# Attention in numbered slots with a written engine order, GLU and branch work moved beside it, and SSM rotations from short tables

## The chip, the cores and the metric

One core of a Trainium2 chip runs the whole kernel. Its engines run side by side, each in the order of its own instruction list: PE (TensorE, matmuls and transposes, with its weight loads shown as PEld), DVE (VectorE), ACT (ScalarE), POOL (GpSimd) and SP, which issues most transfers. The metric is device time in microseconds; a lower time is better. Three runs of the kernel before gave 1538.99 to 1541.56 us, median 1540.11 us.

## The reference, cut to what matters

One decoder layer on 1024 tokens with 16 meta tokens in front (1040 rows of 1024 numbers):

```
xn = RMSNorm(h)
[q | k | v | u | gate_a | gate_b] = xn @ W_in
a  = stick-breaking attention(q, k, v)          8 heads x 64, strictly causal
s  = GLU(S5 complex-diagonal SSM(u))            32 groups x 16 channels, state 64
h += (sigmoid(gate_a) * (a @ W_pa) + sigmoid(gate_b) * (s @ W_pb)) @ W_o
h += hierarchical MoE(RMSNorm(h))               top-1 of 4 groups, then top-2 of 8 experts
```

The attention weight of key s for query t is `sigmoid(z[t,s])` times the product of `1 - sigmoid(z[t,j])` over the keys j between them, with `z = q.k / 8`. The SSM state turns by a fixed complex factor at each step; the kernel works on chunks of 8 tokens (130 chunks), and needs the cosines and sines of 129 multiples of an angle for each state.

## The kernel before

**Numbers.** A matrix product is taken in three passes: each operand is split into a rounded part and the rest (`h` and `l`), and `mm3` (L131) issues `wh*xh`, `wh*xl` and `wl*xh` for each block of 128 contraction rows (L134 to L136). `split` (L101, L102) makes the two parts, the first on ACT, the second on DVE.

**Stages.** The program's order is: norms and transposes of x; the projection of u; the SSM in four blocks of 8 groups (`ssm`); four pairs of heads (`att_proj`, `att_pair`); GLU and the two branches; the output projection with the router; the MoE; the final norm. The gate projections (`gates`, 16 units of 128 columns, two steps of 24 matmuls each) depend on nothing but xn and serve as filler. `weave` alternates two generators by count: 21 gate steps (`SF`) beside the SSM, then projections of the next head pair and 3, 3 and 2 gate steps beside a pair of heads. Beside the last pair stand the GLU steps. This is the order in which instructions are recorded; a list scheduler then places them on each engine by its own estimate of when each could run, so neighbours in the code need not be neighbours on the engine.

**SSM.** For each block POOL builds the tables `RC` and `RS` (128 partitions x 8 groups x 129) by doubling: seven rounds of six passes (L549 to L554). DVE makes `GT` and `ET` (L558 to L563), PE turns them and multiplies the inputs (L598), DVE rotates the result by `RC`, `RS` (L600 to L603), scans it (L606) and, with POOL (L608), rotates it back (L609 to L611); PE forms the output (L618, L620).

**Attention.** A head takes its queries in four groups (j = 0 to 3) of two blocks of 128. For a block, PE computes the logits in chunks of up to 512 columns with two matmuls each: L745 with `kh`, L746 with `kl`. Both contract over 128 rows: `qs` holds a head's rounded queries in its own 64 rows and the rests in the other 64, and `kh` and `kl` hold the head's 64 rows twice. ACT takes two sigmoids of a chunk (L748, L749), POOL masks the last 128 columns (L751), DVE scans the products (L754) and POOL multiplies (L755). PE turns the weights in blocks (L770), ACT and DVE split them (L780, L781), PE multiplies by the values (L790; L785 in the last pair, which works in plain f32). The 16 meta tokens are a block of their own, so its value matmuls contract over 16 rows.

Of the kernel before, what the change touches and what calls it, by code (L numbers as in the profile page):

```python
# [44 lines left out]
SF, MF, GP = 21, 3, (3, 3, 2)  # L45
# [7 lines left out]
def _f(ap):  # L53
    return ap.bitcast(F32)
# [19 lines left out]
def tile_block(ctx, tc, i, out):  # L74
# [16 lines left out]
    attn_d = dr.tile([512, S], F32, name="attn_d")  # L91
    gate_d = dr.tile([2 * D, S], F32, name="gate_d")
# [46 lines left out]
    with ExitStack() as ca:  # L139
# [21 lines left out]
        with ExitStack() as cx:  # L161
# [5 lines left out]
            def proj(col, chunks, evac):  # L167
                h, l = load_w([win[:, :, col:col + 128]])
                for n0, n1 in chunks:
                    t = ps.tile([128, 512], F32, name="mm", bufs=2)  # L170
                    for k in range(KD):
                        mm3(t[:, :n1 - n0], h[:, k, :], l[:, k, :], xh[:, k, n0:n1], xl[:, k, n0:n1], k == 0, k == KD - 1)
                    evac(t, n0, n1)
                    yield

# [94 lines left out]
            aq = [None, pool(c3, "aq1", bufs=2)]  # L270
            cq = ExitStack()
            aq[0] = pool(cq, "aq0", bufs=2)
            st = {}
            drain(islice(gen, MF), att_proj(tc, ap, aq[0], ps, proj, ident, 0, st))
            for hp in range(3):
                pair = att_pair(tc, ap, ps, ident, hp, st, attn_d)
                fill = chain(att_proj(tc, ap, aq[(hp + 1) % 2], ps, proj, ident, hp + 1, st), islice(gen, GP[hp]))
                weave(pair, fill, 16, 8 + GP[hp])
                drain(fill, pair)
            dst = []  # L280
            pair = att_pair(tc, ap, ps, ident, 3, st, attn_d, dst)
            next(pair)
            drain(gen)
            cq.close()


        with ExitStack() as c4:
            c5 = ExitStack()
            p = pool(c5, "br", side="right")
            ah, al, sh, sl = (p.tile([128, 4, S], F32R, name=n) for n in ("ah", "al", "sh", "sl"))  # L290
            with ExitStack() as c6:
                nc.sync.dma_start(gb, i["glu_b"])
                at = pool(c6, "glu", bufs=2, side="right")
                gl = glu(tc, at, ps, i, load_w, mm3, split, gb, y_d, sh, sl)

                def loads():
                    for k in range(3):
                        a = wp.tile([128, 2, 512], F32, name="wr", bufs=2)
                        nc.sync.dma_start(a, attn_d[k * 128:k * 128 + 128])
                        split(ah[:, k], al[:, k], a.rearrange("p a b -> p (a b)"))  # L300
                        yield
                dst += ah, al
                weave(pair, chain(gl, loads()), 16, 18)
                drain(pair, gl)
# [25 lines left out]
            wa = i["w_branch_attn"].rearrange("(k p) c -> p k c", p=128)  # L330
            wb = i["w_branch_ssm"].rearrange("(k p) c -> p k c", p=128)
            w0 = load_wo(0)
            p = pool(c5, "gat", side="right", bufs=2)
            for m in range(KD):
                h, l = load_w([wb[:, :, m * 128:m * 128 + 128], wa[:, :, m * 128:m * 128 + 128]])
                T2 = []
                for q in range(2):
                    c = slice(q * 512, q * 512 + 512)
                    t = ps.tile([128, 512], F32, name="qk", bufs=2)
                    for k in range(4):  # L340
                        mm3(t, h[:, k, :], l[:, k, :], sh[:, k, c], sl[:, k, c], k == 0, k == 3)
                    T2.append(t)
                for q in range(2):
                    c = slice(q * 512, q * 512 + 512)
                    ga = p.tile([128, 512], F32, name="ga")
                    gb = p.tile([128, 512], F32, name="gb")
                    nc.sync.dma_start(gb, gate_d[D + m * 128:D + m * 128 + 128, c])
                    nc.sync.dma_start(ga, gate_d[m * 128:m * 128 + 128, c])
                    V.tensor_mul(gb, gb, T2[q])
# [4 lines left out]
                    P.tensor_add(ga, ga, gb)  # L354
# [15 lines left out]
def ssm_prep(tc, p, i, bcast, out):  # L370
# [72 lines left out]
    t1, t2 = W("t1", (128, 4, G)), W("t2", (128, 4, G))  # L443
# [18 lines left out]
    for _ in range(3):  # L462
# [4 lines left out]
        V.tensor_scalar(s, wi, 2.0, None, op0=OP.mult)  # L467
    yield
# [22 lines left out]
    X, X2, C1, C2, BA, BB, u1 = (W(n, (128, G, CH)) for n in ("X", "X2", "C1", "C2", "BA", "BB", "u1"))  # L491
# [20 lines left out]
    out.update(c=c, s=s, Lr=Lr, Li=Li, d8=d8, BA=BA, BB=BB, C1=C1, C2=C2, sg=sg, nsg=nsg, dd=dd)  # L512


def ssm(tc, p, ps, ident, u_d, y_d, prep):
    nc = tc.nc
    V, A, P = nc.vector, nc.scalar, nc.gpsimd
    c, s, Lr, Li, d8, BA, BB, C1, C2, sg, nsg, dd = (
        prep[n] for n in ("c", "s", "Lr", "Li", "d8", "BA", "BB", "C1", "C2", "sg", "nsg", "dd"))
# [4 lines left out]
    N = NCH - 1  # L524
    for blk in range(4):
# [12 lines left out]
        RC, RS = W("RC", (128, 8, N), bufs=2), W("RS", (128, 8, N), bufs=2)  # L538
        P.memset(RC[:, :, 0:1], 1.0)
        P.memset(RS[:, :, 0:1], 0.0)  # L540
        P.tensor_copy(RC[:, :, 1], c[:, gs])
        P.tensor_copy(RS[:, :, 1], s[:, gs])
        ta, tb = W("ta", (128, 8, 64)), W("tb", (128, 8, 64))
        n = 1
        while n < 128:
            br, bi = (x[:, :, n:n + 1].to_broadcast([128, 8, n]) for x in (RC, RS))
            ar, ai = RC[:, :, 1:n + 1], RS[:, :, 1:n + 1]
            a, b = ta[:, :, :n], tb[:, :, :n]
            P.tensor_mul(a, ai, bi)  # L549
            P.tensor_mul(b, ar, br)  # L550
            P.tensor_sub(RC[:, :, n + 1:2 * n + 1], b, a)
            P.tensor_mul(a, ar, bi)
            P.tensor_mul(b, ai, br)
            P.tensor_add(RS[:, :, n + 1:2 * n + 1], a, b)  # L554
            n *= 2
        yield
        GT, tmp, ET = W("GT", (128, 8, T + 1, CH), bufs=2), W("tmp", (128, 8, T + 1, CH)), W("ET", (128, 8, T, CH), bufs=2)
# [14 lines left out]
        KP = W("KP", (CH, 8, 2, 128))  # L572
        P.memset(KP[:, :, 0], 0.0)
        for g0 in (0, 4):
# [4 lines left out]
            A.copy(KP[:, g0:g0 + 4, 1], tp[:CH])  # L579
        dg = W("dg", (CH, 8, CH))  # L580
        V.tensor_mul(dg, dd[:, gs, None].to_broadcast([CH, 8, CH]), ident[:CH, None, :CH].to_broadcast([CH, 8, CH]))
        V.tensor_add(KP[:, :, 1, 0:CH], KP[:, :, 1, 0:CH], dg)
        M = W("M", (128, 8, 128), bufs=2)
        KPf = KP.rearrange("p g a b -> p g (a b)")
        for ti in range(T):
            nc.sync.dma_start(M[ti * CH:ti * CH + CH], KPf[:, :, 128 - CH * ti:256 - CH * ti])
# [45 lines left out]
def glu(tc, p, ps, i, load_w, mm3, split, gb, y_d, sh, sl):  # L632
    nc = tc.nc
    V, A, P = nc.vector, nc.scalar, nc.gpsimd
    yh = p.tile([128, 4, S], F32R, name="yh", bufs=1)
    yl = p.tile([128, 4, S], F32R, name="yl", bufs=1)
    yd = y_d.rearrange("f t c -> f (t c)")

    def load(k, q):
        y = p.tile([128, 512], F32, name="y", bufs=2)  # L640
        nc.sync.dma_start(y, yd[k * 128:k * 128 + 128, q * 512:q * 512 + 512])
        return y

    for k in range(4):
# [757 lines left out]
```

## Time and profile before

| | us |
|---|---|
| median of three runs | 1540.11 |
| the profiled execution: its own time | 1539.6 |
| the profiled execution: its span | 1537.7 |
| SSM beside gate projections | 73.2 to 262.9 |
| head pairs | 262.9 to 653 |
| branches | to 725 |
| output projection, router, MoE, final norm | 725 to 1537.7 |

PE is recorded as busy in 1456.8 us (95%) of the span, DVE in 63%, ACT in 47%, POOL in 34%. A matmul's recorded duration runs on into the next one's, so busy time alone says little: the distance between the starts of two equal neighbours is what one costs. The granted clock is 1.0 at 2.4 GHz; a stretch with a mean below that was partly at 1.2 GHz.

### The profile page before, as it was taken

Reading aid. Unit: us, or ns where it says so; the run is one execution under the profiler, and the core shown is the slowest. Engines: PE = TensorE matmul, PEld = TensorE weight load, DVE = VectorE, ACT = ScalarE, POOL = GpSimd, SP = SyncE. Lnnn points to the kernel's source line nnn. Section 1 sums busy time; section 2 is a strip of 40 time slices with the busy share of each in tenths; the row PEclk is TensorE's granted clock in tenths of the full one; section 3 lists DMA queues with packets and bytes.
Section 4 is the critical chain, followed back from the end, with each engine's and each line's share of the span. In section 5 each row is a group of like instructions: output and inputs, shape, how many; then the busy total and the mean of one; then the engine's idle time right before and its main releaser. Section 6 shows DMA issues by size and latency. Waiting matters only on the chain. (4 is left out here: it accounts for less than half of the span.)

```text
span 1537.7 us, 19509 instructions
## 1 busy us (share of the span) xinstructions
PE 1456.8 (95%) x6900; PEld 1123.4 (73%) x6900; DVE 963.0 (63%) x1488; ACT 722.3 (47%) x1141; POOL 518.9 (34%) x542
## 2 busy tenths in 40 slices
PE   7989799999999989999998799999999999999986
PEld 6967688998888867778787566666666666666663
DVE  6757565465756568665578566666665566656547
ACT  6212122455656577432223255555555455555543
POOL 1199941144444465332255321111111111111034
PEclk8999899999999999999999799999999999999998
DMA  8242344211111015264763799999999989999754
GB/s 256 77 104 72 92 104 97 60 42 54 30 51 34 28 44 142 78 198 160 268 247 124 286 346 356 352 354 353 356 360 351 353 342 358 334 334 357 271 200 163
DMA packets 132197, 314.77 MB, mean 205 GB/s; under 512 B 24305, under 2 KB 82289, under 8 KB 107522
## 3 DMA queue, kind: packets, MB, share of 16 engines
q1 hardware_dynamic: 120898, 295.99, 55.0%
q0 software_dynamic: 9728, 16.83, 2.9%
q8 instruction: 55, 0.90, 0.2%
q10 hardware_dynamic: 1472, 0.69, 0.2%
q14 instruction: 44, 0.36, 0.1%
HBM read 284.03 MB, written 44.11 MB: 213 GB/s over the span
## 5 line engine op out<-in xcount | busy, mean ns | idle before, releaser
L134 PE MATMUL mm<-xh,wh 128*128 128x512 f32 (+4 forms) x608 | 224.1, 369 | 1.1 <-DVE kl L691 0.6
L135 PE MATMUL mm<-xl,wh 128*128 128x512 f32 (+4 forms) x608 | 222.6, 366 | 0.0
L136 PE MATMUL mm<-xh,wl 128*128 128x512 f32 (+4 forms) x608 | 221.3, 364 | 0.8 <-DVE wl L102 0.8
L1159 POOL DMA_INDIRECT ye_d<-w,tab x32 | 56.1, 1754 | 250.0 <-ACT w L1152 249.4
L134 PEld LDWEIGHTS mm<-xh,wh 128*128 128x128 f32 x608 | 115.4, 190 | 16.0 <-issue 1.1
L136 PEld LDWEIGHTS mm<-xh,wl 128*128 128x128 f32 x608 | 115.4, 190 | 14.9 <-DVE wl L102 1.5
L135 PEld LDWEIGHTS mm<-xl,wh 128*128 128x128 f32 x608 | 115.3, 190 | 13.9 <-DVE xl L225 0.4
L754 DVE TENSOR_TENSOR_SCAN pr<-pr 128x144 f32<-128x144 f32 (+3 forms) x64 | 92.6, 1448 | 46.8 <-POOL pr L751 46.1
L102 DVE TENSOR_TENSOR w<-m,w 128x2048 fp32r<-128x2048 f32 x38 | 88.9, 2342 | 40.8 <-ACT w L101 40.7
L102 DVE TENSOR_TENSOR w<-r,w 128x2048 fp32r<-128x2048 f32 x36 | 82.2, 2291 | 47.6 <-ACT w L101 47.2
L1066 POOL DMA_INDIRECT w<-hg_d,tab x31 | 34.8, 1122 | 222.0 <-PE tr L1088 217.1
L755 POOL TENSOR_TENSOR be<-be,pr 128x143 f32<-128x143 f32 (+3 forms) x64 | 89.4, 1400 | 38.4 <-DVE pr L754 36.0
L1120 PE MATMUL a<-r,xf 128*128 128x512 f32 x224 | 100.7, 592 | 0.0
L1120 PE MATMUL a<-m,xf 128*128 128x512 f32 x208 | 93.3, 592 | 0.0
L1128 DVE SCALAR_TENSOR_TENSOR mid<-a,tab,mid 128x512 f32<-128x512 f32 x64 | 47.9, 749 | 63.8 <-ACT mid L1126 52.0
L101 ACT CAST w<-r 128x2048 fp32r<-128x2048 f32 x38 | 72.1, 1903 | 27.5 <-PE a L1113 14.4
L101 ACT CAST w<-m 128x2048 fp32r<-128x2048 f32 x38 | 72.5, 1907 | 18.9 <-PE o L1146 10.3
L101 ACT CAST wh<-wr 128x1024 fp32r<-128x1024 f32 (+1 forms) x44 | 44.6, 1014 | 65.8 <-PE mm L135 57.3
L1120 PEld LDWEIGHTS a<-r,xf 128*128 128x128 f32 x224 | 41.8, 190 | 42.3 <-issue 40.4
L102 DVE TENSOR_TENSOR wl<-wr,wh 128x1024 fp32r<-128x1024 f32 (+1 forms) x44 | 57.1, 1297 | 23.6 <-ACT wh L101 23.5
L1146 PE MATMUL o<-w,w 128*128 128x512 f32 x172 | 68.6, 399 | 3.2 <-DVE w L102 3.2
L751 POOL TENSOR_SCALAR_AFFINE_SELECT pr<-pr 128x128 f32<-128x128 f32 x64 | 26.3, 411 | 132.9 <-ACT pr L748 113.1
(534 smaller groups left out, 3766.2 us busy)
## 6 DMA issues: line engine op xcount, KB each, us to landing
r<-in_w_dram SPq DMA_DIRECT2D x84, 1024.0 KB, 7.9
m<-in_w_dram SPq DMA_DIRECT2D x82, 1024.0 KB, 8.1
x<-in_w_dram SPq DMA_DIRECT2D x26, 1024.0 KB, 7.9
wr<-in_w_in_dram SPq DMA_DIRECT2D x32, 512.0 KB, 4.2
gate_d<-gt SPq DMA_DIRECT2D x32, 256.0 KB, 2.3
x<-in_x_dram SPq DMA_DIRECT2D x8, 512.0 KB, 4.6
y<-y_d SPq DMA_DIRECT2D x16, 256.0 KB, 3.2
wr<-in_w_out_dram SPq DMA_DIRECT2D x8, 512.0 KB, 4.3
```

The source lines that it names most:

```text
L101: a = (A if heng is None else heng).copy(h, src)
L102: return a.ins, (V if leng is None else leng).tensor_sub(l, src, _f(h)).ins
L134: nc.tensor.matmul(ps, lhsT=wh, rhs=xh, start=first, stop=False)
L135: nc.tensor.matmul(ps, lhsT=wh, rhs=xl, start=False, stop=False)
L136: nc.tensor.matmul(ps, lhsT=wl, rhs=xh, start=False, stop=last)
L754: V.tensor_tensor_scan(rv, rv, rv, 1.0, op0=OP.mult, op1=OP.bypass)
L755: P.tensor_mul(be[:, :W - 1], be[:, :W - 1], pr[:, 1:W])
L1066: q = P.indirect_dma_start(out=xg[e % XG], out_offset=None, in_=hg_d, in_offset=IO(ap=tab[:, e, 0:1] if e else rt["idx"], axis=0), bounds_ ...
L1120: nc.tensor.matmul(a[w], lhsT=xf[:, k], rhs=raws[n][:, k], start=False, stop=(k == 3))
L1128: V.scalar_tensor_tensor(s, a[n], r, s, op0=OP.mult, op1=OP.mult)
L1146: nc.tensor.matmul(o[n], lhsT=hh[:, kk], rhs=l[:, k, cs], start=False, stop=False)
L1159: put = P.indirect_dma_start(out=ye_d, out_offset=IO(ap=tab[:, e, 1:2], axis=0), in_=y, in_offset=None, bounds_check=2 * S - 1, oob_is_err ...
```

## The change

- **Rotations.** Two short tables of powers (17 and 9 entries for all 32 groups) are made once on DVE (`powers`); each block's `RC` and `RS` of 9 x 16 entries are their products: three passes on POOL and three on DVE. The block matrix `M` is loaded above its diagonal blocks only, into two pages cleared at the start.
- **Filler.** 20 gate steps stand beside the SSM instead of 21.
- **Slots.** Attention, GLU and the remaining gates are recorded by `attention` in 122 slots (numbers -10 to 111; the 112 from 0 on handle one block of value matmuls each). In a slot PE turns the next block, computes up to two logit chunks, takes a quota of filler and multiplies a block by the values; ACT, DVE and POOL work on what the slots before have left (`later`). Inside `manual_schedule` the four engines keep the recorded order; SP does not belong to it.
- **Plan.** GLU runs in slots -3 to 8 beside the first heads and leaves its result in DRAM (`s_d`); projections and gates fill slots up to 97; in slot 98 the pages of xn are given up and `s_d`, `attn_d` are read back into pages made there; slots 104 to 111 take the SSM half of two of the eight branch units.
- **Keys.** `kl` holds each head's 64 rows once; the second logit matmul contracts over these 64 rows alone, with the rounded queries.

```diff
-SF, MF, GP = 21, 3, (3, 3, 2)
+SF = 20
+AHEAD = 2
...
+        plan = [((-10, -4), [unit_qkv(0, 2)]), ((-3, 8), [unit_glu(m) for m in range(4)]), ((9, 24), qkv(1)),
+                ((25, 52), [unit_gate(10)] + qkv(2)), ((53, 80), [unit_gate(m) for m in (11, 12)] + qkv(3)),
+                ((81, 97), [unit_gate(m) for m in (13, 14, 15)]), ((104, 111), [unit_branch(m) for m in range(AHEAD)])]
...
+            for k in range(4):
+                sl.later(1 + k, lambda k=k: load_s(s_d, *late["s"], k, 128))
+            for k in range(4):
+                sl.later(6 + k, lambda k=k: load_s(attn_d, *late["a"], k, 128 if k < 3 else 64))
...
+        with tc.manual_schedule(engines={mybir.EngineType.PE, mybir.EngineType.Activation, mybir.EngineType.DVE, mybir.EngineType.Pool}):
+            attention(heads, sl, range(-10, 112), quota, fill, {98: merge_pages}, attn_d)
...
+    pb = powers("pb", 16, c, s)
+    pa = powers("pa", 8, pb[0][:, :, 16], pb[1][:, :, 16])
...
-        while n < 128:
-            br, bi = (x[:, :, n:n + 1].to_broadcast([128, 8, n]) for x in (RC, RS))
-            ar, ai = RC[:, :, 1:n + 1], RS[:, :, 1:n + 1]
-            a, b = ta[:, :, :n], tb[:, :, :n]
-            P.tensor_mul(a, ai, bi)
-            P.tensor_mul(b, ar, br)
-            P.tensor_sub(RC[:, :, n + 1:2 * n + 1], b, a)
...
+        for eng, R, t, x, y, op in ((V, RS, tb, (ar, bi), (ai, br), OP.add), (P, RC, ta, (ar, br), (ai, bi), OP.subtract)):
+            eng.tensor_mul(R, *x)
+            eng.tensor_mul(t, *y)
+            eng.tensor_tensor(R, R, t, op=op)
...
-                        nc.tensor.matmul(z[:, :c1 - c0], lhsT=q, rhs=k1[e][:, c0:c1], start=True, stop=False)
-                        nc.tensor.matmul(z[:, :c1 - c0], lhsT=q, rhs=k2[e][:, c0:c1], start=False, stop=True)
...
+        nc.tensor.matmul(z[:, :c1 - c0], lhsT=q, rhs=self.k1[e][:, c0:c1], start=True, stop=False)
+        nc.tensor.matmul(z[:, :c1 - c0], lhsT=q[own], rhs=self.k2[own, c0:c1], start=False, stop=True)
...
+        sl.later(1, sigmoids)
+        if last:
+            sl.later(2, scan)
...
+    for x in slots:
+        sl.now = x
+        if x in at:
+            at[x]()
+        store = None
+        if 0 <= x + 1 < len(blocks):
+            s, b = blocks[x + 1]
+            h, e, j = steps[s]
+            store = h.turn(e, j, b)
+        sl.run()
+        if store:
+            store()
+            w[x + 1] = h.w
+        for h, *z in zs.get(x, []):
+            h.logits(*z, sl)
+        for _ in range(quota.get(x, 0)):
+            next(fill)
+        if 0 <= x < len(blocks):
+            s, b = blocks[x]
+            h, e, j = steps[s]
+            h.values(e, j, b, w.pop(x))
```

POOL's list in the SSM stage before: the last round of doubling of the first block's tables (`ta`, `tb` are scratch), then the next block's first passes.

```order
L549 TENSOR_TENSOR ta_932<-RS_927 128x512
L550 TENSOR_TENSOR tb_933<-RC_926 128x512
L551 TENSOR_TENSOR RC_926<-tb_933,ta_932 128x8x64
L552 TENSOR_TENSOR ta_932<-RC_926,RS_927 128x512
L553 TENSOR_TENSOR tb_933<-RS_927,RC_926 128x512
L554 TENSOR_TENSOR RS_927<-ta_932,tb_933 128x8x64
L549 TENSOR_TENSOR ta_1300<-RS_1295 128x8
L550 TENSOR_TENSOR tb_1301<-RC_1294 128x8
```

POOL's list in the same stage now; `par`, `pai`, `pbr`, `pbi` are the short tables, `R` with `St` the rotation back of a block's scan.

```order
L668 TENSOR_TENSOR RC_983<-par_554,pbr_524 128x1152
L668 TENSOR_TENSOR RC_1275<-par_554,pbr_524 128x1152
L669 TENSOR_TENSOR ta_985<-pai_555,pbi_525 128x1152
L670 TENSOR_TENSOR RC_983<-RC_983,ta_985 128x1152
L628 TENSOR_TENSOR u1_607<-X_603,fi_581 128x512
L669 TENSOR_TENSOR ta_1277<-pai_555,pbi_525 128x1152
L670 TENSOR_TENSOR RC_1275<-RC_1275,ta_1277 128x1152
L669 TENSOR_TENSOR ta_1575<-pai_555,pbi_525 128x1152
L722 TENSOR_TENSOR R_1138<-St_1140,RC_983 128x1032
```

42 table passes of a block have become three, and the second block's tables stand ahead of the first block's rotation.

PE's list before, where the third head pair ends: logit chunks (`qk`) stand between value matmuls (`pv`) and transposes (`tr`) where the scheduler put them.

```order
L745 MATMUL qk_5840<-kh_4739,qs_4737 128x264
L746 MATMUL qk_5840<-kl_4741,qs_4737 128x264
L790 MATMUL pv_5633<-wth_5676,V_3722 128x256
L745 MATMUL qk_5929<-kh_4739,qs_4737 128x328
L746 MATMUL qk_5929<-kl_4741,qs_4737 128x328
L790 MATMUL pv_5633<-wtl_5677,V_3722 128x256
L790 MATMUL pv_5633<-wth_5676,V_3722 128x256
```

PE's list now, one slot among the first heads: the last transposes of a block, two logit chunks, filler.

```order
L914 MATMUL tr_2889<-ident_60,be_2631 128x128
L914 MATMUL tr_2889<-ident_60,be_2680 128x128
L880 MATMUL qk_2914<-kh_2151,qs_2149 128x272
L881 MATMUL qk_2914<-kl_2152,qs_2149 128x272
L880 MATMUL qk_2919<-kh_2151,qs_2149 128x400
L881 MATMUL qk_2919<-kl_2152,qs_2149 128x400
L136 MATMUL mm_2932<-xh_85,wh_2834 128x512
L137 MATMUL mm_2932<-xl_86,wh_2834 128x512
```

The row of L881 now lies alone between matmuls over 128 rows, in all 112 logit chunks of the program.

PE's list now in slots 99 to 101, where the plan has no filler.

```order
L880 MATMUL qk_6182<-kh_4899,qs_4897 128x456
L881 MATMUL qk_6182<-kl_4900,qs_4897 128x456
L880 MATMUL qk_6185<-kh_4899,qs_4897 128x456
L881 MATMUL qk_6185<-kl_4900,qs_4897 128x456
L946 MATMUL pv_6154<-wth_6143,V_4901 128x128
L914 MATMUL tr_6189<-ident_60,be_5977 128x128
L914 MATMUL tr_6189<-ident_60,be_6016 128x128
```

Before, the GLU's matmuls stood among the chunks of these last heads.

## Rows read from the trace of the kernel before

**Rows 1.** The page's first part: busy us, share of the span, instructions.

```profile
PE 1456.8 (95%) x6900; PEld 1123.4 (73%) x6900; DVE 963.0 (63%) x1488; ACT 722.3 (47%) x1141; POOL 518.9 (34%) x542
```

**Rows 2.** Busy time by stage: length, each engine's busy us, clock, DMA.

```profile
73.20:262.90 189.70, 171.48 (x854) 140.76 (x854) 120.31 (x156) 41.98 (x65) 134.37 (x197) 0.94 0.41 97
262.90:540.00 277.10, 274.32 (x1616) 241.56 (x1614) 168.56 (x251) 156.20 (x378) 109.14 (x132) 1.00 0.15 42
540.00:660.00 120.00, 110.10 (x551) 85.52 (x550) 84.10 (x93) 73.87 (x181) 60.32 (x63) 0.97 0.31 91
660.00:726.00 66.00, 66.00 (x292) 54.25 (x291) 40.74 (x62) 17.17 (x35) 18.84 (x15) 1.00 0.55 176
870.00:1480.00 610.00, 604.72 (x2378) 413.21 (x2376) 367.81 (x252) 340.91 (x312) 92.73 (x65) 1.00 0.90 337
```

**Rows 3.** PE's waits in the SSM stage: us in total, times, longest.

```profile
PE qk L618 <- DVE R L611: 11.3, 2, 10.0
PE qk L598 <- DVE mm__1124 L602: 6.9, 1, 6.9
```

**Rows 4.** Busy time in 20 us of the SSM stage.

```profile
100.00:120.00 20.00, 13.06 (x59) 10.46 (x59) 8.26 (x14) 1.17 (x2) 18.12 (x36) 0.77 0.37 77
```

**Rows 5.** POOL's costliest lines, 60 to 263 us: busy us, mean ns, idle before.

```profile
L551 POOL TENSOR_TENSOR RC<-tb,ta 128x8 f32<-128x8 f32 (+6 forms) x28 | 21.6, 773 | 2.0
...
L552 POOL TENSOR_TENSOR ta<-RC,RS 128x8 f32<-128x8 f32 (+6 forms) x28 | 16.6, 593 | 2.0
L608 POOL TENSOR_TENSOR R<-St,RC 128x1032 f32<-128x1032 f32 x4 | 11.6, 2911 | 35.7 <-DVE St L606 35.7
```

**Rows 6.** DVE lines, 54 to 263 us.

```profile
L600 DVE TENSOR_TENSOR R<-qk,RC 128x387 f32<-128x387 f32 (+1 forms) x12 | 6.1, 510 | 14.3 <-POOL RC L551 8.5 <-PE qk L598 5.7
...
L560 DVE TENSOR_TENSOR GT<-GT,tmp 128x1152 f32<-128x1152 f32 x4 | 5.9, 1474 | 0.0
...
L398 DVE SCALAR_TENSOR_TENSOR ea<-ea,eq 128x32 f32<-128x32 f32 x12 | 2.3, 191 | 0.1
```

**Rows 7.** PE in order of time: start us, us, line, contracted*output rows, form.

```profile
472.06 0.40 PE L134 MATMUL mm<-xh,wh 128*128 128x512 f32 x1
472.29 0.40 PE L135 MATMUL mm<-xl,wh 128*128 128x512 f32 x1
472.62 0.38 PE L790 MATMUL pv<-wth,V 16*128 16x256 f32 x1
472.93 0.50 PE L136 MATMUL mm<-xh,wl 128*128 128x512 f32 x1
473.26 0.40 PE L134 MATMUL mm<-xh,wh 128*128 128x512 f32 x1
```

**Rows 8.** PE's weight loads in the same stretch.

```profile
472.06 0.19 PEld L135 LDWEIGHTS mm<-xl,wh 128*128 128x128 f32 x1
472.62 0.18 PEld L790 LDWEIGHTS pv<-wth,V 16*128 16x128 f32 x1 [0.36 <-issue]
```

**Rows 9.** PE in order of time, value matmuls over 128 rows, then transposes.

```profile
466.99 0.28 PE L790 MATMUL pv<-wth,V 128*128 128x256 f32 x1
467.11 0.28 PE L790 MATMUL pv<-wtl,V 128*128 128x256 f32 x1
...
467.63 1.36 PE L770 MATMUL tr<-ident,be 128*16 128x128 f32 x11
```

**Rows 10.** Weight loads of the second logit matmul, 263 to 660 us.

```profile
L746 PEld LDWEIGHTS qk<-kl,qs 128*128 128x128 f32 x112 | 21.4, 192 | 0.9
```

**Rows 11.** ACT lines of the attention, 263 to 660 us, shapes apart.

```profile
L101 ACT CAST wh<-wr 128x1024 fp32r<-128x1024 f32 x18 | 19.0, 1056 | 12.1 <-PE mm L135 10.8 <-issue 1.2
...
L748 ACT ACTIVATE pr<-qk 128x456 f32<-128x456 f32 x16 | 8.9, 557 | 4.3 <-PE qk L746 4.1
L748 ACT ACTIVATE pr<-qk 128x392 f32<-128x392 f32 x16 | 8.1, 505 | 1.8 <-POOL be L755 0.8 <-PE pv L790 0.5 <-PE qk L746 0.4
...
L778 ACT COPY wth<-tr 128x512 f32<-128x512 f32 x12 | 6.7, 576 | 6.6 <-PE tr L770 6.6
```

**Rows 12.** The page's DMA issues: count, KB each, us to landing.

```profile
wr<-in_w_in_dram SPq DMA_DIRECT2D x32, 512.0 KB, 4.2
```

## What the change should do to the time

> **What bounds the kernel now.** I read the page's first part, then busy time by stage, then in the stages where PE is not full the waits, then single instructions in order of time. The first part names PE: recorded as busy in 1456.8 of 1537.7 us, with DVE next at 963.0 [rows 1]. A matmul's record runs on into its successor, so this share hides what is lost; the table by stage shows it better [rows 2]. From 262.9 to 540 us PE is idle for 277.1 - 274.3 = 2.8 us, from 660 to 726 for nothing. From 870 to 1480 us the DMA share is 0.90 at 337 GB/s; that stretch belongs to the MoE, which the change leaves alone. Two stretches have slack: the SSM stage, 73.2 to 262.9 us, with 171.5 busy of 189.7 and a granted clock of 0.94, and the last heads, 540 to 660 us, with 110.1 busy of 120 and 0.97.
>
> So the kernel is a list of PE instructions with two weak places. The change works on both, and it also adds something to PE in the place where PE is full.
>
> What PE needs is counted from starts: 512-wide neighbours start 472.29 - 472.06 = 0.23 us apart [rows 7], 256-wide ones 0.12 apart, and eleven 128-wide transposes take 1.36, 0.12 each [rows 9].
>
> **SSM stage: about 17 us less.** The stage holds 565 matmuls 512 wide (by the code, 504 of them are its gate steps) and 288 narrow instructions. I take 0.231 and 0.112 for their paces, means over many neighbours that agree with the rows above: 565 x 0.231 + 288 x 0.112 = 162.7 us. The stage takes 189.7, so 27 us are lost. PE's waits name 11.3 + 6.9 = 18.2 of them, all on DVE's rotations [rows 3]; the rest is low clock, as from 100 to 120 us, where PE is busy for 13.1 of 20 us at a granted clock of 0.77 [rows 4]: between the two levels, 1.2 and 2.4 GHz, after PE had waited. DVE in its turn waits for POOL's `RC` (8.5 us before L600 [rows 6]). POOL's tables are therefore what is late: six lines, 28 instructions each, from 0.59 to 0.77 us [rows 5], together 113.6 of POOL's 134.4 us there [rows 2].
>
> In the order now these 168 passes are 12 on POOL and 12 on DVE [the two POOL lists above]. A pass over 128x1152 took 1.47 us on DVE [rows 6]; on POOL 128x1032 took 2.9 [rows 5], so 3.2 for 1152. POOL falls to 134.4 - 113.6 + 12 x 3.2 = 59 us of 189.7 and is no longer late. DVE gains 12 x 1.45 = 17 and some 50 small instructions for `powers` at 0.19, the row of 32 elements [rows 6], 10 us: 120.3 + 27 = 147. One filler step fewer and a re-cut of the steps bring 36 matmuls 512 wide out of the stage and into the attention, which is neutral (8.3 us each way); the stage's PE need is then 154.4. So DVE at 147 stands under PE at 154, both run in order, and PE still waits for DVE at the block ends. The bounds are all 27 regained, and only the table wait removed with the 17 + 10 us of new DVE work showing in part, 5 regained. I take 10 of the 27 as staying: -17.
>
> The half page `kl` saves 24 subtractions on DVE beside the heads, DVE is at 168.6 of 277.1 there [rows 2]; the round trip of `s_d` lies under the pairs' filler, with a DMA share of 0.15. Both count nothing while PE leads by that much; if DVE led, the first would be a gain of 24 x 0.5 = 12 us.
>
> **The second logit matmul over 64 rows: about 41 us more.** Columns and passes stay the same; only the contraction becomes 64 rows between matmuls over 128 [the list of one slot]. No row of before has a 64-row matmul between wide ones, so the price is bounded. From below: its weight load costs what it cost before, hidden, 0.9 us idle before all 112 [rows 10], and the price is 0. A gain I exclude, since the columns streamed are the same. From above and nearest: the 16-row value matmul between 128-row ones. Starts run 472.29, 472.62, 472.93, 473.26 [rows 7]. From the last full-row matmul before it to the second behind it pass 0.97 us; at pace the three steps are 0.23 + 0.12 + 0.23 = 0.58. So one excursion to fewer rows costs 0.39 us, half going in and half coming out. The weight loads say why: a load beside full-row neighbours starts with the matmul ahead of it, while the 16-row load starts at 472.62 with its own matmul, after 0.36 us of idle time ended by nothing but issue [rows 8]. The 64-row load is the same event with another number, so I take the upper end. 112 x 0.39 = 43.7; of the 112 chunks, seven lie in slots 98 to 102, where PE waits for ACT anyway (below): 105 x 0.39 = +41.
>
> The Trainium skill has a rule on each side of this. "TensorEngine Tiling (Array Packing)", Key Properties: "Changing tiling mode (not just tile) drains the TensorE"; 64 and 32 rows are modes of their own there, and by that rule every chunk pays. "TensorE: Matmul & The Clock Gate", Step-by-step, lets a weight load be pulled ahead of matmuls in flight when its row groups don't conflict or when it goes to a background buffer; by that the chunk would pay nothing. The 0.36 us before the 16-row load agrees with the first and speaks against the second; no row shows 64 rows.
>
> **Slots with filler (-10 to 97): about 0.** In such a slot PE has 2.6 to 3.5 us of work by the paces above, ACT 2.0 to 2.3, DVE 2.0 to 2.4 and POOL 1.5: two chunks on ACT are four sigmoids at 0.51 to 0.56 and a block's copy at 0.58 [rows 11]. PE stays the bound, and each product is asked for a slot after the work that made it. What the fixed order can add is a wait of ACT or DVE for a weight page: 4.2 us from issue to landing [rows 12], and the cast waiting for it (L101, 1.06 us [rows 11]) has the next sigmoids queued behind it. I take 0; the upper bound is in the rivals.
>
> **The end of the heads: about 0.** Slots 98 to 103 have no filler: the list shows logits, values and transposes alone. ACT has there 8.8 us of sigmoids (chunks of 328 to 456 columns, two each), 4 casts of branch weights at 1.05, some 3.2 of block copies and a gate sigmoid of 0.6: 16.8 us. PE has 9.6, or 12.3 with the seven excursions. PE idles for about 7 us, and the low clock that follows such idle time before [rows 4] costs perhaps 3. Then slots 104 to 111 need two pages, a landing of 4.2 us and a split of 1.05 + 1.3 each, some 4 us late. That is 14 us lost. The old end loses 9.9 idle + 3 % of 120 in clock = 13.5 [rows 2], up to 18.6 against the paces. The two cancel; the bounds are -13 (nothing idle) and +12 (casts late as well). The two branch units moved here are taken out of the branches, where PE is full [rows 2], and neutral but for that.
>
> **The sum**, against the profiled execution's 1539.6 us (span 1537.7 and 1.9 around it; the median of the runs is 0.5 higher): 1539.6 - 17 + 41 + 0 + 0 = 1563.6, in round figures 1563. Its bounds without the excursions' price: -27 to -5, and -13 to +12 at the end, taken together about +-18: 1545 to 1580.
>
> **The rivals.**
> - *The 64-row load is pulled ahead like a full one* (112 loads, 0.9 us [rows 10]): the price is 0 and the sum 1539.6 - 17 = 1522. For it: a 16-row load may be a different case from 64. Against: the rows of the 16-row load. If SSM and end give more, 1512.
> - *The written order stalls.* ACT or DVE reach an instruction for a page that has not landed, and the chunks queued behind it hold PE in the next slot. 108 slots with filler take about 20 units, each with a page of 4.2 us; about 1 us late each time is +20, 1583, with the excursions. It decides from the point where a page is asked for less than 4.2 us, two slots, ahead. Against: PE has 2.6 to 3.5 us a slot to ACT's 2.3, so late work catches up.
> - *Half the price*: only one of the two changes of row count shows, 0.2 us each, 105 x 0.2 = 21: 1539.6 - 17 + 21 = 1543, no change that can be measured or slightly slower.
> - *Price real, but both weak places heal*: 27 in the SSM and 18 at the end, 1539.6 + 41 - 45 = 1536.
> - *Not what it says*: the tables still hold DVE, since half of the passes move onto it and POOL's are long; then the first term is -5, 1576, inside the forecast's range.
>
> **How the numbers follow.** Forecast 0.58; 64 rows free 0.18; stalls 0.10; half price 0.08; both heal 0.06. Executions differ by about 0.1 %, so 0.2 % (3 us) is the smallest change to tell. Faster: 0.18 of the free load, 0.04 of the healing, 0.02 of the half price and of the forecast's lower end, 0.24. Same: 0.06. Slower: 0.70. The range reaches down to the free load's 1521 and up to the stalls' 1583; half of each of these lies beyond, 0.14 in all. The likeliest case alone: 1545 to 1580.
>
> **What would show it.** In the profile of the changed kernel: weight loads of L881 recorded over 64 rows, with idle time "issue" ahead of nearly each, and starts of the matmuls round them 0.2 us later than the pace on either side; the stretch of the heads some 40 us longer at equal work. The SSM stage ending at 235 to 245 us, POOL no longer named in DVE's waits there, the granted clock near 1.0. PE waiting for ACT's sigmoids in slots 98 to 103 and nowhere before. I am wrong if L881's loads start with the matmul ahead of them, or if ACT and DVE show waits for weight pages that end PE's idle time among the heads.

## The result, and the profile after

The changed kernel takes 1590.62 us (median of 4 runs, 1589.97 to 1591.68) against 1539.55 us: ratio 1.033, 95% interval 1.0312 to 1.0348, 51 us slower. The sign was forecast; the time lies above the upper end of the range, 1583.

The page's first part, in the form of [rows 1]:

```profile
PE 1498.5 (94%) x6900; PEld 1137.3 (72%) x6900; DVE 984.3 (62%) x1515; ACT 727.4 (46%) x1134; POOL 421.2 (26%) x368
```

PE issues the same 6900 matmuls and is recorded as busy for 42 us more; POOL's work fell by 98 us, DVE's rose by 21. Where the time went is seen at three marks, start times on PE in each trace:

| us | before | after |
|---|---|---|
| last output matmul of the SSM | 262.7 | 256.4 |
| first logit matmul | 285.0 | 283.9 |
| first matmul of the output projection | 725.1 | 777.2 |
| from there to the last matmul | 797.9 | 797.5 |

All of the loss lies ahead of the output projection. One thing has to be kept in mind: work was moved. The SSM stage has 36 wide matmuls (8.3 us) less, and the three gate steps behind it are gone from there too; against that, more of the projections stand ahead of the heads. Up to the first logit matmul PE has 96 matmuls of 512 columns less and 63 of 272 to 384 more, some 12 us less at their paces. So the heads begin 1.1 us sooner with 12 us less done, and then take 493.3 us instead of 440.1 with those 12 us in them: about 11 us are lost ahead of the heads and 41 in them.

Busy time by stage, columns as in [rows 2]: the SSM stage, the stretch behind it, two of the heads, the end of the heads.

```profile
73.20:256.60 183.40, 165.68 (x829) 135.16 (x828) 162.89 (x210) 40.45 (x62) 56.41 (x25) 0.96 0.35 91
256.40:283.90 27.50, 20.01 (x118) 19.58 (x116) 11.38 (x18) 12.30 (x23) 0.00 (x0) 0.88 0.31 77
300.00:400.00 100.00, 98.70 (x532) 80.51 (x530) 66.00 (x89) 56.37 (x132) 35.63 (x46) 1.00 0.28 79
650.00:670.00 20.00, 16.98 (x62) 10.79 (x62) 11.84 (x9) 14.95 (x36) 10.52 (x11) 0.83 0.54 187
670.00:700.00 30.00, 27.06 (x110) 21.34 (x111) 11.61 (x11) 8.94 (x15) 2.56 (x1) 0.83 0.26 79
```

In the SSM stage POOL is down from 134 us to 56, near the 59 worked out. But DVE is up from 120 to 163 instead of 147, and PE still misses 17.7 of 183.4 us. Behind it, from 256 to 284 us, PE loses 7.5 us more; before, it lost 2.8 us in all from 262.9 to 540 [rows 2]. The clock is below 1.0 in both.

PE's waits, first from 73 to 257 us, then from 257 to 777 us (us in total, times, longest):

```profile
PE qk L732 <- DVE R L725: 8.0, 2, 4.1
PE mm L138 <- DVE wl L104: 4.5, 1, 4.5
PE tr L685 <- DVE ET L679: 3.3, 1, 3.3
PE qk L712 <- DVE Y L740: 1.9, 1, 1.9
...
PE mm L136 <- DVE qs L830: 7.0, 1, 7.0
PE pv L946 <- DVE al L955: 5.6, 3, 2.9
PE pv L946 <- DVE ao L962: 5.1, 6, 2.6
PE qk L136 <- DVE gb L410: 2.2, 1, 2.2
```

Every wait of the SSM stage is still one for DVE, but no instruction of DVE waits for a table now (compare [rows 3, 6]): DVE itself is late. Behind the SSM a wait of 7.0 us for the first query pages is new, and in the heads there are nine for the copies of a finished query group out of PSUM (`ao`, `al`), where before there was one of 0.5 us.

Two logit chunks on PE in order of time, columns as in [rows 7], and the weight loads beside them:

```profile
305.15 0.45 PE L880 MATMUL qk<-kh,qs 128*128 128x456 f32 x1
305.53 0.47 PE L881 MATMUL qk<-kl,qs 64*128 64x456 f32 x1
305.93 0.48 PE L880 MATMUL qk<-kh,qs 128*128 128x456 f32 x1
306.34 0.47 PE L881 MATMUL qk<-kl,qs 64*128 64x456 f32 x1
306.75 0.51 PE L136 MATMUL mm<-yh,wh 128*128 128x512 f32 x1
```

```profile
305.53 0.18 PEld L881 LDWEIGHTS qk<-kl,qs 64*128 64x128 f32 x1 [0.21 <-issue]
305.93 0.19 PEld L880 LDWEIGHTS qk<-kh,qs 128*128 128x128 f32 x1 [0.22 <-ACT wth L929]
306.34 0.18 PEld L881 LDWEIGHTS qk<-kl,qs 64*128 64x128 f32 x1 [0.22 <-issue]
306.74 0.19 PEld L136 LDWEIGHTS mm<-yh,wh 128*128 128x128 f32 x1 [0.22 <-issue]
```

A 456-wide step took 0.205 us where neighbours contract over the same rows; each of the four here takes 0.38 to 0.41. A weight load on either side of a row change starts with its own matmul and not with the one ahead of it. The group of all 112 loads, to be read against [rows 10] (0.9 us idle there):

```profile
L881 PEld LDWEIGHTS qk<-kl,qs 64*128 64x128 f32 x112 | 20.6, 184 | 18.8 <-issue 15.3
```

By median starts of the 456-wide chunks the step from L880 to L881 takes 0.39 and the step behind L881 0.40 us, against 0.205: 0.38 together, near the 0.39 that the 16-row matmul had given.

Why DVE got 163 us, in order of time: DVE first, then POOL.

```profile
93.95 0.69 DVE L624 TENSOR_TENSOR BA<-X,fr 128x512 f32<-128x512 f32 x1
104.20 3.35 DVE L675 TENSOR_TENSOR tmp<-C,Li 128x1152 f32<-128x1152 f32 x1
107.47 3.15 DVE L629 TENSOR_TENSOR BB<-BB,u 128x512 f32<-128x512 f32 x1
110.55 3.19 DVE L104 TENSOR_TENSOR wl<-wr,wh 128x1024 fp32r<-128x1024 f32 x1
113.66 1.34 DVE L676 TENSOR_TENSOR GT<-GT,tmp 128x1152 f32<-128x1152 f32 x1
```

```profile
103.16 3.17 POOL L669 TENSOR_TENSOR ta<-pai,pbi 128x1152 f32<-128x1152 f32 x1
106.41 3.66 POOL L670 TENSOR_TENSOR RC<-RC,ta 128x1152 f32<-128x1152 f32 x1
110.15 2.50 POOL L669 TENSOR_TENSOR ta<-pai,pbi 128x1152 f32<-128x1152 f32 x1
```

A product of 512 columns takes 0.69 us at 93.95, just ahead of a POOL pass that starts at 94.00, and 3.15 us at 107.47, begun while POOL works on one; a product of 1152 takes 1.34 alone and 3.35 begun beside POOL; the three slow ones end 1.2, 0.6 and 1.1 us behind the POOL pass that they met (ends at 106.33, 110.07 and 112.65), about what they take alone. The Trainium skill ("SBUF — State Buffer", Who interferes with whom) has the rule: a DVE instruction that reads two operands from SBUF contends with a GpSimd instruction that reads SBUF, and one of the two waits for the whole of the other. The rows agree. The trace of before had held the warning, which the forecast did not read: two of DVE's four L610 lasted 1.34 and 1.56 us, the other two 3.39 and 3.38, with POOL's L608 beside them.

```profile
L610 DVE TENSOR_TENSOR mm__2166<-St,RS 64x1032 f32<-64x1032 f32 x1 | 3.4, 3387 | 0.0
...
L610 DVE TENSOR_TENSOR mm__1124<-St,RS 64x1032 f32<-64x1032 f32 x1 | 1.3, 1344 | 0.0
```

### The profile page after: what moved, and what is told of

It is laid out like the page before. It is cut to its first block, busy times and chain, and to the rows that moved or that the text cites. A ratio compares the mean times of both kernels' runs of the same rounds, so it can differ in the third digit from the quotient of the medians.

```text
span 1590.0 us, 19411 instructions
## 1 busy us (share of the span) xinstructions
PE 1498.5 (94%) x6900; PEld 1137.3 (72%) x6900; DVE 984.3 (62%) x1515; ACT 727.4 (46%) x1134; POOL 421.2 (26%) x368
## 5 line engine op out<-in xcount | busy, mean ns | idle before, releaser
L136 PE MATMUL mm<-xh,wh 128*128 128x512 f32 (+4 forms) x608 | 230.9, 380 | 7.6 <-DVE qs L830 7.0
L137 PEld LDWEIGHTS mm<-xl,wh 128*128 128x128 f32 x608 | 116.4, 191 | 12.8 <-DVE xl L238 1.1
L895 DVE TENSOR_TENSOR_SCAN pr<-pr 128x144 f32<-128x144 f32 (+3 forms) x64 | 89.0, 1400 | 18.8 <-POOL pr L890 18.5
L930 DVE TENSOR_TENSOR wtl<-tr,wth 128x512 fp32r<-128x512 f32 (+3 forms) x108 | 51.3, 476 | 57.2 <-ACT wth L929 56.8
L946 PE MATMUL pv<-wth,V 128*128 128x256 f32 (+2 forms) x240 | 72.6, 354 | 10.8 <-DVE al L955 5.6
L929 ACT CAST wth<-tr 128x512 fp32r<-128x512 f32 (+3 forms) x108 | 45.2, 419 | 65.9 <-PE tr L914 50.5
L890 POOL TENSOR_SCALAR_AFFINE_SELECT pr<-pr 128x128 f32<-128x128 f32 x64 | 29.1, 454 | 174.0 <-ACT pr L886 172.2
```

Source lines behind the costliest of these rows:

```text
L136: nc.tensor.matmul(ps, lhsT=wh, rhs=xh, start=first, stop=False)
L137: nc.tensor.matmul(ps, lhsT=wh, rhs=xl, start=False, stop=False)
L895: V.tensor_tensor_scan(rv, rv, rv, 1.0, op0=OP.mult, op1=OP.bypass)
L930: V.tensor_sub(wl[:n, s, q], tp[:n, s, q], _f(wh[:n, s, q]))
L946: nc.tensor.matmul(self.po[:, cols], lhsT=h.rearrange("p a b -> p (a b)"), rhs=_f(x) if self.native else x, start=first and r == 0, stop=l ...
```

## The experiments

Fourteen kernels. "Full rows" means the second logit matmul over 128 rows; intervals are those of the ratio to the kernel before in the same runs.

**1. Full rows in the changed kernel.**

```diff
-lhsT=q[own], rhs=self.k2[own, c0:c1]
+lhsT=q, rhs=self.k2[:, c0:c1]
```

> The changed kernel, its second logit matmul over all 128 rows again: the query page against the half page of keys as it stands, so that the product of the two remainders is one head's with the other's (the size of a rounding error). Same columns, same instructions, no row change. Theory (a step to 64 rows and back costs 0.386 us, 0.196 going in and 0.195 coming out, as the starts around L881 show): 112 x 0.386 = 43 us less, some of it lost where PE waits anyway, 1547 to 1551 us. Rival (the price is an effect of the written order, whose waits fill the time again): 1585 to 1591 us.

Measured 1561.52 us, ratio 1.0134 (1.0115 to 1.0152): 29.1 us less, between the theory's 43 and the rival's 0. The steps themselves went: the same 112 loads have 0.1 us idle before them.

```profile
L881 PEld LDWEIGHTS qk<-kl,qs 128*128 128x128 f32 x112 | 21.6, 193 | 0.1
```

But PE's idle time in the heads grew by about 11 us. Its waits from 257 us on:

```profile
PE pv L946 <- DVE ao L962: 10.8, 8, 3.0
PE mm L136 <- DVE qs L830: 7.0, 1, 7.0
PE pv L946 <- DVE al L955: 6.6, 3, 3.3
```

So the price per chunk is about right and the time is not its product: a faster PE waits longer for the others. The two traces can be laid side by side, since from the first logits to the last PE runs the same 1937 instructions in the same order. Where neither waits the changed kernel needs 40.3 us more, 0.36 a chunk; where one of them waits run 1 needs 10.1 us more. The price falls on three steps: 0.09 us on the one into L881 (0.18 between two chunks), 0.19 on the one behind it and, where no chunk follows, 0.10 on the next. That is another division than the expectation's 0.196 and 0.195, with nearly the same sum. What it waits for, ACT and DVE at one such place (start, us):

```profile
547.87 1.06 ACT L103 CAST wh<-wr 128x1024 fp32r<-128x1024 f32 x1
548.95 0.37 ACT L961 COPY ao<-pv 64x256 f32<-64x256 f32 x1
```

```profile
548.96 1.23 DVE L104 TENSOR_TENSOR wl<-wr,wh 128x1024 fp32r<-128x1024 f32 x1 [1.20 <-ACT wh L103]
550.10 0.41 DVE L962 TENSOR_TENSOR ao<-pv,ao 64x256 f32<-64x256 f32 x1
```

The copy of the group's result, 0.37 + 0.41 us, stands behind the split of a weight page on both engines, and the next group's first value matmul stands behind the copy. Of the eight waits for `ao`, two (4.6 us) end behind such a split and four (5.1 us) behind the writing of key pages on DVE.

**2. The 64 rows alone, in the kernel before** (half a page `kl`, L746 over 64 rows).

> The kernel before with one edit of the change: a half page of keys and 64 rows in the second logit matmul; 24 subtractions on DVE fewer. Theory (the row change alone makes the heads longer, whatever sets the order): 1540 + 43 = 1583 us, down to 1575 if the scheduler's order lets two chunks stand next to each other or some lie in idle time. Rival (the cost needs the written order): 1535 to 1545 us.

Measured 1566.44 us, ratio 1.0168 (1.0151 to 1.0185): 27 us more. It needs no written order, but again some of the 43 us is missing: the scheduler's PE waited 11.7 us in the heads before and 3.2 here, about half of what is missing. The edit also takes 24 subtractions from DVE.

**3. Two chunks share one step.**

```diff
-nc.tensor.matmul(z[...], lhsT=q[own], rhs=self.k2[own, c0:c1], ...)
+self.second.append(lambda: nc.tensor.matmul(z[...], lhsT=q[own], ...))
...
+while h.second:                   # behind all logits of the slot
+    h.second.pop(0)()
```

> The changed kernel; where a slot holds two logit chunks, both first matmuls are issued and then both second ones, so that two chunks share one step to 64 rows and back. Theory (the price is for the change of row count, 0.386 us there and back, not for a matmul of 64 rows): 31 slots have two chunks (31 starts from L881 to the next L880), 31 x 0.386 = 12 us less PE time, of which the run with full rows gave back about a third as waits: 1578 to 1584 us. Rival (a 64-row matmul is slow wherever it stands): 1589 to 1592 us.

Measured 1583.10 us, ratio 1.028: 7.5 us less, as the theory has it with a third given back. The traces say it directly: the four steps of two 456-wide chunks take 1.20 us here and 1.59 in the changed kernel, one price of 0.39 less with the same two matmuls of 64. The price belongs to the change of rows, not to a matmul of 64.

**4. All six table passes on DVE.**

```diff
-... (P, RC, ta, (ar, br), (ai, bi), OP.subtract)):
+... (V, RC, ta, (ar, br), (ai, bi), OP.subtract)):
```

> The changed kernel with all six table passes of a block on DVE, none on POOL: 12 passes of 1.36 us more for DVE, 16 us. Theory (a DVE instruction that meets a POOL pass takes as long as that pass, 3.15 us where it alone takes 1.2 to 1.4; some 25 us of DVE's 163 in the SSM stage): DVE falls by 5 to 15 us there, since part of the meetings is with the rotation back that stays on POOL, and the time by 3 to 12, 1579 to 1588 us. Rival (DVE's work is what counts, and it gets 16 us more): 1598 to 1607 us.

Measured 1581.84 us, ratio 1.0267: 8.8 us less, though DVE has 16 us more to do. Its busy time from 73.2 us to the SSM's last output matmul fell all the same, from 163 to 154 us, as the theory has it. By count of work alone it would have been slower.

**5. Short tables alone, in the kernel before** (`ssm_prep` and `ssm` of the changed kernel, nothing else).

> The kernel before with the SSM part of the change alone: short tables on DVE, three passes on POOL and three on DVE for each block's tables, the block matrix in cleared pages; all else as before, 21 filler steps. The forecast's first term: 17 us less, 1522 us. Theory now (DVE instructions wait out the long POOL passes, so DVE becomes the late engine in place of POOL): -5 to +5 us, 1535 to 1545 us.

Measured 1534.25 us, ratio 0.9956 (0.9942 to 0.997): 5.8 us less, just beyond the theory's -5 and far from -17.

**6. The same with all of the SSM's POOL work on DVE** (also L722 and the two products L625, L628).

```diff
-    P.tensor_mul(u1, X2, b16(fi))
+    V.tensor_mul(u1, X2, b16(fi))
...
-        P.tensor_mul(R, St, RC)
+        V.tensor_mul(R, St, RC)
```

> The kernel before with short tables, and everything that POOL does in the SSM (three table passes a block, the rotation back, two products ahead) given to DVE. Theory (DVE is held up by POOL's passes more than it is by the same work of its own; all six table passes on DVE brought 9 us in the changed kernel): 1534 - 8 to 14 = 1520 to 1526 us. Rival (DVE is at its limit in this stage, 12 + 4 + 2 passes of 1.3 us more): 1540 to 1555 us.

Measured 1529.01 us, ratio 0.9914 (0.9892 to 0.9937): 5 us less than run 5, short of the 8 to 14. In its stage the effect is whole. From 73.2 to 252.8 us, run 5 and then this run:

```profile
73.20:252.80 179.60, 167.57 (x829) 136.44 (x828) 162.32 (x210) 41.09 (x64) 56.26 (x23) 0.96 0.37 95
```

```profile
73.20:252.80 179.60, 179.60 (x916) 147.82 (x915) 151.69 (x222) 44.73 (x68) 0.34 (x2) 1.00 0.38 101
```

DVE runs 12 instructions more in 10.6 us less (over the whole of the SSM's own lines 18 more, 157.4 us against 167.2), PE has no idle time left and the granted clock is 1.0. What follows gives part of it back:

```profile
PE mm L134 <- DVE qs L701: 7.0, 1, 7.0
```

This is the changed kernel's wait for the first query pages. PE, no longer stopped in the SSM, has used up the filler by the time of the last block's end: at its last output matmul (252.9 us, 257.8 in run 5) it has done 14 us more of matmuls.

**7. Run 5 without the three gate steps behind the SSM.**

```diff
-SF, MF, GP = 21, 3, (3, 3, 2)
+SF, MF, GP = 21, 0, (4, 4, 3)
```

> The kernel before with short tables, but without the three gate steps behind the SSM (they lie beside the head pairs instead: 4, 4 and 3). Theory (in the changed kernel the heads begin 12 us later than in this one by equal work, since no filler lies beside the SSM's last block): the start of the heads 3 to 10 us later by equal work, PE waiting for the first query pages as the changed kernel does; 1537 to 1546 us. Rival (the wait is of the changed kernel's order alone): 1532 to 1536 us.

Measured 1555.30 us, ratio 1.0098 (1.0081 to 1.0114): 21 us more than run 5, more than foreseen. The changed kernel's wait appears:

```profile
PE mm L134 <- DVE qs L701: 6.9, 1, 6.9
```

Between the two profiled runs, the longest of run 5 and the shortest of this one, the spans differ by 15.8 us, and 14.5 of them lie ahead of the output projection: by equal work 5 ahead of the first logits, as the theory has it, and 9 in the heads and branches, which it did not foresee.

**8 and 9. More filler at that place in the changed kernel**: gate unit 10 out of slots 25 to 52, once as `SF = 22`, once recorded behind the SSM.

```diff
-SF = 20
+SF = 22
...
-((25, 52), [unit_gate(10)] + qkv(2))
+((25, 52), qkv(2))
```

> The changed kernel with 22 filler steps beside the SSM instead of 20, the gate unit taken out of slots 25 to 52. Theory (PE is out of filler from 247 us on and waits 4.1 us for the last rotation and 7.0 us behind the last block's gelu, with 10 us of low clock after them): 48 matmuls of 11 us lie in that time, 1578 to 1584 us. Rival (DVE's chain, which the filler's split lengthens by one more page, sets the end of the stage): 1588 to 1593 us.

> The changed kernel with gate unit 10 (two steps) recorded right behind the SSM, ahead of the first pair's query and key projections, instead of in slots 25 to 52. Theory (the 7.0 us wait at 263.7 us, and the 6.8 us of low clock that go with it, come from PE having nothing beside the last block's gelu but projections whose pages that block still holds): the wait goes and 11.1 us of matmuls lie under it; the heads begin 0 to 4 us later but need 11.1 us less: 1579 to 1585 us. Rival (the scheduler takes these steps earlier, as it did with 22 filler steps, and the wait stays): 1588 to 1595 us.

Measured 1595.27 us (1.036) and 1593.88 us (1.0351): 3 to 5 us slower, against both theories; the second lies in its rival's range. With 22 steps the wait stays 7.0 us; the output projection begins 3 us sooner (774.0), and the profiled run then loses 5 us behind it. Why is open; that last stretch took 811.7 to 817.5 us over the traces of all sixteen kernels. Recorded behind the SSM the steps shorten the wait to 4.3 us, but the heads, 11.1 us of matmuls shorter, take just 3 us less: up to the last logits the time at low clock rises from 16.7 to 27.3 us. Filler taken out of the slots seems to be missed there.

**10. Five steps behind the SSM in the kernel before, with the edits of runs 6 and 12.**

> The kernel before with short tables, the SSM's POOL work on DVE, the meta block over 128 rows, and five gate steps behind the SSM instead of three (two beside each of the first three pairs). Theory (the wait of 7.0 us for the first query page at 260 us, which is still there, is want of filler behind the SSM): two steps, 11 us, lie under it, 1508 to 1515 us against 1517.9. Rival (the filler only moves away from the pairs, which then wait, or the wait is for the page and any filler before it is used up sooner): 1516 to 1530 us.

Measured 1519.44 us (0.9864) against 1517.87 in run 12: no gain, the rival holds. The wait is 4.3 us.

**11. The copy of a finished group at the head of its slot, full rows.**

```diff
+x.insert(0 if head else len(x), f)
...
-sl.later(1, lambda h=h, e=e, j=j, po=h.po: h.output(e, j, po, attn_d))
+sl.later(1, lambda h=h, e=e, j=j, po=h.po: h.output(e, j, po, attn_d), True)
```

> The changed kernel with the second logit matmul over 128 rows, and in the written order the copy of a finished query group out of PSUM (L955 to L962) at the head of its slot's list on ACT and DVE instead of at its end. Theory (of 41 us that PE saves without the 64 rows 11 come back as waits of the first value matmul of a group for these copies, 10.8 + 6.6 us in all, because they are queued behind the slot's sigmoids and scan): 8 to 15 us less than the 1561.5 us of the run with full rows alone, 1547 to 1554 us. Rival (ACT as a whole is late, and the sigmoids now pushed back make PE wait in their turn): 1558 to 1566 us.

Measured 1576.86 us, ratio 1.0238: 15 us slower than run 1, the rival and worse. The wait for `ao` falls from 10.8 to 0.9 us, and another takes its place:

```profile
PE qk L881 <- ACT be L888: 19.0, 22, 2.1
...
PE pv L947 <- DVE ao L963: 0.9, 1, 0.9
```

ACT now stands in front of a result that PE has not finished (19 of the 24 copies wait for PE, 24 us in all), with the slot's sigmoids behind it.

**12. The meta tokens' block over 128 rows, on top of run 6** (page 8 of `V` cleared, 128 columns turned).

```diff
-n = 128 if kt < 8 else NM
+n = 128
...
+P.memset(Vf[:, 8] if hp == 3 else _f(Vt[:, 8]), 0.0)
```

> As the one before it in this list, with the 16 meta tokens' block of values contracted over 128 rows (the page of values cleared behind its 16 rows, 128 columns turned), so that no matmul of the heads is over fewer rows. Theory (a step to 16 rows and back costs 0.39 us, as read from the trace of before): 32 of them, 12.5 us of PE, most or two thirds of it in time: 8 to 12 us less than the run beside it. Rival (these steps lay in idle time): 0 to 3 us.

Measured 1517.87 us, ratio 0.9856 (0.984 to 0.9873): 11.1 us less than run 6. This is the fastest version, faster than both kernels. The edit also joins the small copies of that block on ACT and DVE with larger ones, so not all of the 11 us need be the steps.

**13. The slots without the written order, full rows.**

```diff
-with tc.manual_schedule(engines={PE, Activation, DVE, Pool}):
+if True:
```

> The changed kernel with the second logit matmul over 128 rows, its slots recorded as they are but without the manual schedule: the list scheduler places them on PE, ACT, DVE and POOL. Theory (in the written order PE stands behind the copies of a finished query group, 17 us of waits for DVE's ao and al): they shrink, 1545 to 1555 us against 1561.5. Rival (the slots' order is as good as the scheduler's, and what is lost in the heads is the work itself): 1558 to 1566 us; or the scheduler fares worse with it: above.

Measured 1549.00 us, ratio 1.0044 (1.0026 to 1.0061): 12.5 us less than run 1. The waits for `ao` are gone, `al` keeps 1.2 us, and the wait for the first query pages has grown from 7.0 to 12.0 us.

**14. All edits in the changed kernel** (runs 1, 6, 12 and 13).

> The changed kernel with every cost found so far taken out: 128 rows in the second logit matmul and in the meta block, the SSM's POOL work on DVE, slots recorded but placed by the list scheduler. Theory (the changed kernel's loss is these terms and the filler missing behind the SSM): 1549 - 9 to 14 - 8 to 12 = 1523 to 1532 us, above the 1517.9 of the kernel before with the same edits by the filler alone. Rival (the slots themselves are worse than the weave of pairs by more): 1533 to 1545 us.

Measured 1526.87 us, ratio 0.991 (0.9893 to 0.9926): as forecast, faster than the kernel before, 9 us behind run 12. Its wait behind the SSM has grown to 12.4 us.

## Why the prediction was right in sign and wrong in size

The runs give a ledger from 1540 to 1590.6, against a forecast of 1563:

| part | forecast | measured | from |
|---|---|---|---|
| short tables | -17 | -5.8 | run 5 |
| filler, slots and end of the heads, written order | 0 | +27.3 | 1561.5 - 1534.25 (runs 1, 5) |
| 64 rows | +41 | +29.1 | 1590.6 - 1561.5 (run 1) |

The misses partly cancel: the first two rows cost 38 us more than forecast, the last 12 us less. The sign was right by luck as much as by its reason. Without the 64 rows the forecast was -17 and the runs say +21.5, slower as well.

The traces divide the middle row. Count as lost what the time exceeds PE's matmuls at the distance of equal neighbours (an estimate, one trace for each run). Run 1 then loses 7 us more than run 5 up to the SSM's last output matmul, 9 more from there to the first logits and 10 more in the heads and branches.

**The price of the row change held, its sum did not.** 0.39 us per chunk was read from another instruction and measured as 0.36 to 0.39. The step that failed is "PE stays the bound": 112 x 0.39 = 43.7 us counts in full only if PE never waits in the heads. In both orders about a third of it did not show in the time (runs 1, 2, 3). Of the 14.6 us missing in run 1 waits make up 10 and the mean price of 0.36 most of the rest; in run 2 waits make up 8.5 of 16.5, and the rest is open. The rival in which the load is pulled ahead is out.

**"SSM stage: about 17 us less"** failed in the term for DVE, 120.3 + 27 = 147. Each addend was about right as work. That DVE's time beside long POOL passes is not its work was left out, and it was 163; the stage ended at 256.4 us, not at 235 to 245. The sum's logic (POOL late, then DVE) stood, though the 8.5 us for `RC` were the smaller part of DVE's waits for POOL: it waited 5.4 and 12.8 us for the rotation back (L608), which stood behind the next block's passes. The stage heals when POOL is silent (run 6).

**"Neutral (8.3 us each way)"** failed most, by some 16 us. What DVE holds up does not end sooner for having less filler: the SSM's last output matmul starts at 257.8 us in run 5 and at 256.9 in run 1, with 8.3 us less for PE to do. And the change takes not one filler step but also the three behind the SSM (`MF`), which the text did not name. They had covered the wait for the first query pages. Why these pages come only when the SSM's last block is done was not tried; in the code their pool is opened where the SSM's is closed. Moving steps back cured little (runs 8 to 10), and it seems that no place has filler to spare: that part of the loss is shown in run 7, not repaired.

**"Slots with filler: about 0"** failed by some 10 us. PE's work per slot was compared with ACT's and DVE's as sums, and sums fit. What decides is order within a slot: the copy of a group behind a page's split or the writing of keys, and nothing can pass it; nor does a better place for the copy alone help (run 11). The rival of the stalling order had +20 for pages that land late; the mechanism of queueing was there, with the page's split, and not its landing, in front. The written order alone is worth 12.5 us (run 13). With all other edits equal the changed arrangement stays 9 us behind (runs 12, 14), and by the count above this is no loss of the slots: run 14 loses 22 us more than run 12 ahead of the first logits and 10 us less from there on. Whether the slots' recording or the filler moved into them brings those 10 us is open.

**The end of the heads**: PE idles there, 5.6 us in three waits for the copy `al`, from 650 to 700 us at a clock of 0.83. In two places the copy stands behind DVE's scan or ACT's sigmoids (2.7 us), much as foreseen; in the third, the longest (2.9 us), it stands behind the split of a page of `attn_d` for whose landing ACT had waited 1.6 us. No run isolates the sum.

## What to carry to other kernels

Before halving a contraction, look at what stands beside it: a lone matmul over fewer rows cost 0.36 to 0.39 us here whatever it saved, and contracting over all 128 rows again removed the price (over another head's remainders in run 1, over zeros in run 12). Price work moved between DVE and POOL by the length of the passes that will meet, not by the totals. Do not count work as neutral when it leaves a stage that another engine holds up. Where a kernel's engines are nearly balanced, take neither a cost nor a gain of the leading engine at its full size.

## What the runs showed of the hardware

A DVE pass over two f32 operands that took 1.2 to 1.4 us alone took 3.1 to 3.4 us when it began within a POOL pass of some 3 us (a shorter one, 0.69 alone, took 3.15), and its own time when it began just ahead of one; moving 12 + 4 + 2 passes from POOL to DVE shortened DVE's busy time on the SSM's lines from 167.2 to 157.4 us (runs 5 and 6). A change from 128 to 64 rows and back cost 0.36 us in the mean of 112 chunks (run 1 against the changed kernel), about the 0.39 us that a change to 16 rows and back cost; the weight load at either edge was not pulled ahead (0.2 us idle before it, 18.8 us before the 112 loads of L881 against 0.9 before).
